# A decoder layer on one core: norms of tokens from a second load of x, squared and summed along rows by ScalarE

## The chip, the cores and the metric

One core of a Trainium2 chip runs the whole program. The metric is device time of one execution in microseconds (us), lower is better. The engines are TensorE (PE in the profile, with PEld for its weight loads), VectorE (DVE), ScalarE (ACT), GpSimd (POOL) and SyncE (SP, which here only issues DMAs and loads registers). Each engine works through its own list of instructions in order, and semaphores hold an instruction until what it reads is there and what it overwrites is free.

## The reference, cut to what matters

One decoder layer over a prompt of 1024 tokens and 8 single-token decode sequences, 1024 features. Its first step is an RMS norm of each token and one wide projection; keys, values, queries and gates come out of the projection.

```python
def rms_norm(x, g):
    xf = x.astype(jnp.float32)
    y = xf * lax.rsqrt(jnp.mean(xf * xf, axis=-1, keepdims=True) + EPS)
    return (y * g.astype(jnp.float32)).astype(x.dtype)
...
q, kc, ks, kw, gl, za, pin, zb, u, v, zc = project(rms_norm(xp, norm_pre[l]), w_in[l])
```

The change concerns only the number `mean(xf * xf)` of each token, for the prompt and for the 8 decode tokens.

## The kernel before

Features lie on partitions: `xT` is loaded as eight tiles of 128 features by 1032 tokens (1024 of the prompt and 8 to decode). The projection is made without the norm, and the norm is multiplied in afterwards, by a tile `R` that holds 1/sqrt of each token's mean square in all partitions.

For float32 precision each tile of x is split into two float16 parts, `xh` (ScalarE) and `xl` (VectorE, `split_x`, lines 277 and 278), each weight tile likewise (`split_k`, `split_w`), and three products are added in PSUM, in three chunks of 344 columns (`t_mms`). The program begins with two weight groups side by side, the keys `G_KSK` and `G_KWK`, in the order in which the eight tiles of x arrive (loop at line 412; `k_mms`). They fill `pa[0]`, `pa[1]`, `pf[0]` and `pf[1]`, whose results ScalarE copies to `tk` (line 457). Then come, group by group, the values `G_KSV` (first by name `t2` in the rows below, PSUM `ps2_0`, `ps2_1`, `ps2_2`), `G_KWV` (`ps3`), the queries and so on (`tgroup`). `ps2_0` and `ps2_1` use the PSUM banks of `pf[0]` and `pf[1]`, and split weights (`ws`) have two buffers, so that those of `G_KSV` take the place of those of `G_KSK`.

The sums of squares of before: `sq_x` squares the tiles of x in place, 0, 2, 4, 6 and 7 on ScalarE with the sum on VectorE (lines 287 and 289), and 1, 3, 5 on GpSimd (lines 283 and 285); line 439 adds the two sums. The 128 partitions are added by nine products with a column of ones (line 445, `pq`). From there: `ssq` (VectorE), `rst` by a power of -1/2 (GpSimd, line 450), a diagonal `dg` (VectorE, line 459), two products with ones that bring it to all partitions (`bcast`, `pr`), and ScalarE's copy to `R` (line 474). `R` then multiplies `tk` (line 484, VectorE); `post_k` makes float16 parts and issues DMAs from GpSimd, and `post_v` fills `vh`, clears its rest by a memset on GpSimd (line 508) and has SyncE transpose it by DMA (line 510).

SyncE and GpSimd keep the order in which the program is written (`manual_schedule`); TensorE, VectorE and ScalarE have an order that a scheduler worked out when the program was built. On SyncE, behind the loads of the start and the load of a weight group (line 243), stand 32 loads of page numbers into registers (line 296), then the next weights, the transposing DMA, and the loads of cache pages (`cr`, line 311), which GpSimd, ScalarE, TensorE and VectorE work on next (`dec_cmp`). Tiles named `t32` share five buffers.

Of the kernel before, what the change touches and what calls it, by code (L numbers as in the profile page):

```python
# [17 lines left out]
NT = 1032  # L18
# [32 lines left out]
def tile_hymba(ctx: ExitStack, tc: tile.TileContext, A: dict):  # L51
# [14 lines left out]
    def mm(out, l, r, st, en):  # L66
        nc.tensor.matmul(out, lhsT=l, rhs=r, start=st, stop=en)  # L67
# [148 lines left out]
    def t32(name, shape=None, dt=F32):  # L216
        return W.tile(shape or [128, NT], dt, tag="t32", name=name, bufs=5)
# [28 lines left out]
    def split_w(gi):  # L246
        raw = raws.pop(gi)
        if gi == "vg":
            ws = D.tile([128, 2, 8, 152], F16, tag="vs", name="wsvg", bufs=1)
            parts = ((raw[0], 0, 128), (raw[1], 128, 152))  # L250
        else:
            ws = X.tile([128, 2, 8, 128], F16, tag="ws", name=f"ws{gi}", bufs=2)
            parts = ((raw, 0, 128),)
        for r, a, b in parts:
            S.activation(ws[:, 0, :, a:b], r, AF.Copy, scale=64.0)  # L255
            if "attn" in hold:
                later(3.8)
                G.tensor_scalar(r, r, 64.0, None, ALU.mult)  # L258
                G.tensor_tensor(ws[:, 1, :, a:b], r, ws[:, 0, :, a:b], ALU.subtract)
            else:  # L260
                V.scalar_tensor_tensor(ws[:, 1, :, a:b], r, 64.0, ws[:, 0, :, a:b], ALU.mult, ALU.subtract)
        wsp[gi] = ws
# [14 lines left out]
        S.activation(xh[k], x, AF.Copy, scale=g)  # L277
        V.scalar_tensor_tensor(xl[k], x, g, xh[k], ALU.mult, ALU.subtract)

    def sq_x(k):  # L280
        x = xraw.pop(k)
        if k in (1, 3, 5):
            G.tensor_tensor(acc[1] if k == 1 else x, x, x, ALU.mult)
            if k > 1:
                G.tensor_tensor(acc[1], acc[1], x, ALU.add)
        else:
            S.activation(x if k else acc[0], x, AF.Square)
            if k:
                V.tensor_tensor(acc[0], acc[0], x, ALU.add)

    pgv = {}

# [61 lines left out]


    G.dma_start(cdt, A["cd"])
    acc = [t32("acc0"), t32("acc1")]
    wk = {}
    for gi, pl in ((G_KSK, RW), (G_KWK, D)):
        wk[gi] = (pl.tile([128, 8, 128], F32, tag="raw" if pl is RW else "rawd", name=f"raw{gi}", bufs=1),  # L360
# [40 lines left out]
    def k_mms(g, ws, k):  # L401
        for c in range(3):
            t_mms(g[c], ws, c, k, k == 0, k == 7)
# [8 lines left out]
    for k in range(8):  # L412
        if k == 0:
            split_k(G_KSK, 1, 4)
            split_k(G_KWK, 1, 4)
        if k == 2:
            split_k(G_KSK, 4, 8)
            split_k(G_KWK, 4, 8)
        if k < 7:
            split_x(k + 1)  # L420
        if k > 0:
            sq_x(k - 1)
        if k == 3:
            load_w(G_KSV)
            load_w(G_KWV)
            for q in range(3):
                load_sw(q)
            Y.dma_start(ptt, A["pt"])
        k_mms(g0, wk[G_KSK][1], k)
        if k < 6:  # L430
            k_mms(g1, wk[G_KWK][1], k)
    sq_x(7)
    for h, xx in ((0, xh), (1, xl)):
        for k in range(8):
            G.tensor_copy(xd[:, k, h], xx[k][:, 1024:NT])
    for h in range(2):
        G.tensor_copy(xdr[:, h].rearrange("p k (b h) -> p k b h", h=8),
                      xd[:, :, h].unsqueeze(3).to_broadcast([128, 8, 8, 8]))
    V.tensor_tensor(acc[0], acc[0], acc[1], ALU.add)
    split_w(G_KSV)  # L440
    k_mms(g1, wk[G_KWK][1], 6)
    k_mms(g1, wk[G_KWK][1], 7)
    pq = op.tile([128, 512], F32, tag="o", name="pq")
    for i in range(8):
        mm(pq[:, i:i + 1], acc[0][:, i * 128:i * 128 + 128], one1[:, 0:1], True, True)
    mm(pq[0:8, 8:9], acc[0][:, 1024:NT], one1[:, 0:1], True, True)
    ssd = D.tile([8, 1], F32, name="ssd")
    rsd = D.tile([8, 1], F32, name="rsd")
    V.tensor_scalar(ssq, pq[:, 0:8], 1.0 / 1024, EPS, ALU.mult, ALU.add)
    G.tensor_tensor(rst, ssq, nhalf[:, 0:8], ALU.pow)  # L450
    V.tensor_scalar(ssd, pq[0:8, 8:9], 1.0 / 1024, EPS, ALU.mult, ALU.add)
    G.tensor_tensor(rsd, ssd, nhalf[0:8, 0:1], ALU.pow)
    vnh = C.tile([128, 2, 8, 256], F16, tag="mxp", name="vnh")
    tk = [t32(f"tk{b}") for b in range(2)]
# [11 lines left out]
    Y.dma_start(bstt, A["cx"][:, 384:640])  # L466

    def bcast():
        for q in range(2):
            pr = op.tile([128, 512], F32, tag="o", name=f"pr{q}")  # L470
            mm(pr, one1, dg[:, q * 4:q * 4 + 4].rearrange("p a b -> p (a b)"), True, True)

            def done(q=q, pr=pr):
                S.activation(R[:, q * 512:q * 512 + 512], pr, AF.Copy)
                if q == 1:
                    V.tensor_copy(R[:, 1024:NT], pq[:, 16:24])
                    V.tensor_scalar(rsn, rst, -1.0 / 64, None, ALU.mult)
# [1345 lines left out]
```

## Time and profile before

| what | us |
|---|---|
| three timed runs | 608.07, 604.58, 608.36 (median 608.07) |
| the profiled execution, its own time | 602.71 |
| its span | 600.9 |
| busy: TensorE, VectorE, ScalarE, GpSimd | 537.8, 461.5, 323.9, 213.6 |

The profile is of one execution. Busy times are summed over stages with different limits, so a stage is read by its own rows: what an engine waited for, and which engine came last. Times in the rows count from the start of the span.

### The profile page before, as it was taken

The numbers are of one execution on the slowest core, as the hardware profiler recorded it, in microseconds if no ns is written. First come the engines' busy times: TensorE is split into PE (matmuls) and PEld (weight loads), VectorE is DVE, ScalarE is ACT, GpSimd is POOL, SyncE is SP. The second block draws the span as 40 slices with busy tenths as digits, with TensorE's granted clock in tenths as the row PEclk, the third lists the DMA queues.
The fourth block names the chain that finished last, engine by engine and source line by source line (L and its number), as shares of the span: only waits on it lengthen the run. The fifth ranks groups of instructions, "written<-read, shape, count | busy, mean of one in ns | idle before, by whom it ended". The sixth has DMA issues, their size and how long they took to land.

```text
span 600.9 us, 14161 instructions
## 1 busy us (share of the span) xinstructions
PE 537.8 (89%) x5716; PEld 348.4 (58%) x5716; DVE 461.5 (77%) x803; ACT 323.9 (54%) x576; POOL 213.6 (36%) x149
## 2 busy tenths in 40 slices
PE   5989989889999999989897987978657999999994
PEld 2656655579768998456565645645233644555551
DVE  5986489995785663578988999979978867877652
ACT  6444245464542443477666746657556747665510
POOL 1794288202446000363732566523943010000010
PEclk9999999998999999899998989989678799999998
DMA  8613884454634826289798878698996894996373
GB/s 299 245 35 121 237 223 129 117 158 126 211 131 131 286 73 170 63 137 189 126 192 165 153 145 124 117 143 193 189 237 122 129 218 104 179 212 155 80 158 122
DMA packets 196883, 95.29 MB, mean 159 GB/s; under 512 B 166866, under 2 KB 185714, under 8 KB 196754
## 3 DMA queue, kind: packets, MB, share of 16 engines
q1 hardware_dynamic: 194018, 81.37, 61.8%
q0 software_dynamic: 2656, 12.77, 6.3%
q8 instruction: 44, 0.72, 0.5%
q10 hardware_dynamic: 144, 0.26, 0.1%
q14 instruction: 21, 0.17, 0.1%
HBM read 45.43 MB, written 11.86 MB: 95 GB/s over the span
## 4 chain that ended last, share of the span: by engine, by line
PE 46%; DVE 21%; DMA 12%; issue 8%; SPq 8%; ACT 3%; POOL 1%; DVEq 0%; POOLq 0%; ACTq 0%
PE op L67 13%; PE ps L67 11%; PE s L67 7%; DMA T<-H 6%; PE zps L67 5%; PE O L67 4%; DVE H L1336 3%; DVE P L1326 3%; SPq L296 3%; PE v1ps L67 2%; DMA o_ps_dram<-dsh 1%; DMA xq<-in_xT_dram 1%; ACT H L1330 1%; SPq L318 1%; SPq L311 1%
## 5 line engine op out<-in xcount | busy, mean ns | idle before, releaser
L67 PE MATMUL ps<-xh,ws 128*128 128x344 f16 x768 | 178.4, 315 | 7.1 <-DVE t L492 4.8
L67 PEld LDWEIGHTS <-ws 128*128 128x128 f16 x1376 | 129.7, 100 | 89.8 <-issue 17.9
L1328 ACT ACTIVATE P<-P,sm 128x640 f32<-128x640 f32 (+7 forms) x128 | 92.9, 727 | 73.4 <-DVE sm L1326 73.1
L67 PE MATMUL ps<-xl,ws 128*128 128x344 f16 x384 | 120.9, 315 | 0.0
L1326 DVE CUSTOM_DVE_ANT_0 P<-s,ctt 128x640 f32<-128x640 f32 (+7 forms) x128 | 85.9, 701 | 12.2 <-PE s L67 11.2
L1336 DVE SCALAR_TENSOR_TENSOR H<-P,H 128x1024 f16<-128x1024 f32 (+4 forms) x50 | 83.5, 1670 | 14.5 <-ACT H L1330 14.5
L67 PEld LDWEIGHTS <-qa 128*128 128x128 f16 (+1 forms) x612 | 46.4, 98 | 80.3 <-issue 51.4
L1330 ACT ACTIVATE H<-P 128x1024 f16<-128x1024 f32 (+4 forms) x50 | 66.2, 1326 | 24.5 <-DMA T<-H 23.6
L67 PE MATMUL O<-vn,T 128*128 128x64 f16 x1584 | 61.7, 198 | 14.8 <-DMA T<-H 14.8
L67 PEld LDWEIGHTS <-T 128*128 128x128 f16 x1584 | 56.7, 101 | 24.8 <-DMA T<-H 16.3
L67 PE MATMUL s<-ka,qa 128*128 128x384 f16 (+4 forms) x192 | 54.4, 340 | 14.8 <-DVE sm L1326 14.5
L67 PEld LDWEIGHTS <-xh 128*128 128x128 f16 x768 | 61.3, 99 | 0.7
L67 PE MATMUL op<-wo,qa 128*128 128x512 f16 x192 | 46.1, 387 | 1.5 <-DMA qa<-yza 1.5
L67 PE MATMUL zps<-ws,xh 128*128 128x128 f16 x512 | 45.0, 219 | 0.0
L67 PE MATMUL zps<-ws,xl 128*128 128x128 f16 x256 | 43.6, 219 | 0.0
L1499 POOL TENSOR_SCALAR sq<-sq 128x1 f32<-128x1 f32 x8 | 2.6, 327 | 106.3 <-ACT o L1529 92.9
L67 PEld LDWEIGHTS <-xl 128*128 128x128 f16 x384 | 38.0, 99 | 2.7 <-issue 2.1
L258 POOL TENSOR_SCALAR raw<-raw 128x1024 f32<-128x1024 f32 x6 | 19.1, 3186 | 55.8 <-ACT ws L255 55.7
L67 PE MATMUL s<-kl,qa 64*128 64x384 f16 (+5 forms) x100 | 34.1, 348 | 0.0
L255 ACT ACTIVATE ws<-raw 128x1024 f16<-128x1024 f32 x21 | 22.2, 1056 | 16.4 <-PE ps L67 10.5
L67 PE MATMUL s<-klx,qx 64*128 64x384 f16 (+4 forms) x92 | 30.9, 335 | 0.0
L585 POOL TENSOR_TENSOR cr<-cr,pett 128x512 f32<-128x512 f32 x12 | 23.8, 2005 | 6.7 <-DMA cr<-in_ccmp_dram 6.1
(333 smaller groups left out, 946.3 us busy)
## 6 DMA issues: line engine op xcount, KB each, us to landing
raw<-in_wt_dram SPq DMA_DIRECT2D x21, 512.0 KB, 4.1
wor<-in_wo_dram POOLq DMA_DIRECT2D x8, 512.0 KB, 5.8
xr<-in_xn_dram SPq DMA_DIRECT2D x8, 512.0 KB, 4.4
o_kww_dram<-in_cwin_dram POOLq DMA_DIRECT2D x1, 4088.0 KB, 16.6
o_y_dram<-o SPq DMA_DIRECT2D x7, 512.0 KB, 3.7
cr<-in_ccmp_dram SPq DMA_DIRECT2D x24, 128.0 KB, 3.0
xq<-in_xT_dram SPq DMA_DIRECT2D x3, 516.0 KB, 8.4
kr<-in_cselk_dram SPq DMA_DIRECT2D x20, 64.0 KB, 2.0
```

Source lines behind the costliest of these rows:

```text
L67: nc.tensor.matmul(out, lhsT=l, rhs=r, start=st, stop=en)
L255: S.activation(ws[:, 0, :, a:b], r, AF.Copy, scale=64.0)
L258: G.tensor_scalar(r, r, 64.0, None, ALU.mult)
L296: pgv[n] = Y.value_load(ptt[0:1, n:n + 1], min_val=0, max_val=39)
L311: Y.dma_start(t[:, :, j * 128:(j + 1) * 128], A["ccmp"][page(b, j)].rearrange("o p (r c) -> (o p) r c", r=2))
L318: Y.dma_start(t[:, 0, j * 128:(j + 1) * 128], A["csel" + kv][page(b, j)].rearrange("o p c -> (o p) c"))
L585: G.tensor_tensor(xv, xv, pet[:, r].unsqueeze(1).to_broadcast([128, 8, 64]), ALU.add)
L1326: V.tensor_tensor_reduce(p, ps[:, z:z + T], ctt[:, end - T:end], -slope, 3e38, ALU.add, ALU.min, sm[:, s, br:br + 1])
L1328: S.activation(p, p, AF.Exp, bias=sm[:, s, br:br + 1], scale=-1.0, accum_out=sm[:, s, 2 + br:3 + br])
L1330: S.activation(H[:, 0], P, AF.Copy, scale=1024.0)
L1336: V.scalar_tensor_tensor(H[:, 1], P, 1024.0, H[:, 0], ALU.mult, ALU.subtract)
L1499: G.tensor_scalar(sq[:, 2:3], sq[:, 1:2], 1.0 / 1024, sq[:, 0:1], ALU.mult, ALU.add)
```

## The change

The nine sums of squares come from a second load of x, this time with tokens on partitions (`xn`, 1024 by 1024, and `xs`, 8 by 1024, both in memory already). Nine loads on SyncE fill tiles `xsq` of 128 tokens by 1024 features, taken from the five `t32` buffers, and one instruction of ScalarE per tile squares it and gives the sum of each row (`accum_out`) into a column of `ssn`. The squares of `sq_x`, the additions on VectorE and GpSimd and the nine products with ones are gone, and `ssq` reads `ssn`. The first product of `bcast` is asked for one step later (`yield 0.0`).

```diff
-    def sq_x(k):
-        x = xraw.pop(k)
-        if k in (1, 3, 5):
-            G.tensor_tensor(acc[1] if k == 1 else x, x, x, ALU.mult)
-            if k > 1:
-                G.tensor_tensor(acc[1], acc[1], x, ALU.add)
+    xsq = {}
+
+    def load_n(i):
+        xsq[i] = t32(f"xsq{i}", [128, 1024])
+        if i < 8:
+            Y.dma_start(xsq[i], A["xn"][i * 128:(i + 1) * 128])
         else:
-            S.activation(x if k else acc[0], x, AF.Square)
-            if k:
-                V.tensor_tensor(acc[0], acc[0], x, ALU.add)
+            Y.dma_start(xsq[i][0:8], A["xs"])
+
+    def sq_n(i):
+        t = xsq.pop(i)
+        if i < 8:
+            S.activation(t, t, AF.Square, accum_out=ssn[:, i:i + 1])
+        else:
+            S.activation(t[0:8], t[0:8], AF.Square, accum_out=ssn[0:8, 8:9])
...
-    acc = [t32("acc0"), t32("acc1")]
+    ssn = D.tile([128, 9], F32, name="ssn")
...
-        if k > 0:
-            sq_x(k - 1)
         if k == 3:
...
             Y.dma_start(ptt, A["pt"])
+            for i in range(3):
+                load_n(i)
+        if k > 4:
+            load_n(k - 2)
+            sq_n(k - 5)
...
-    sq_x(7)
...
-    V.tensor_tensor(acc[0], acc[0], acc[1], ALU.add)
     split_w(G_KSV)
+    for i in range(3, 9):
+        if i < 6:
+            load_n(i + 3)
+        sq_n(i)
     k_mms(g1, wk[G_KWK][1], 6)
     k_mms(g1, wk[G_KWK][1], 7)
     pq = op.tile([128, 512], F32, tag="o", name="pq")
-    for i in range(8):
-        mm(pq[:, i:i + 1], acc[0][:, i * 128:i * 128 + 128], one1[:, 0:1], True, True)
-    mm(pq[0:8, 8:9], acc[0][:, 1024:NT], one1[:, 0:1], True, True)
...
-    V.tensor_scalar(ssq, pq[:, 0:8], 1.0 / 1024, EPS, ALU.mult, ALU.add)
+    V.tensor_scalar(ssq, ssn[:, 0:8], 1.0 / 1024, EPS, ALU.mult, ALU.add)
...
     def bcast():
+        yield 0.0, None
         for q in range(2):
```

What the scheduler made of it on ScalarE, from the last split of x (`xh7`) to the first copies of `G_KSV`'s results; `ws2` and `ws3` are the split weights of `G_KSV` and `G_KWV`, and what an instruction waits for stands in brackets. Before:

```order
L277 ACTIVATE xh7_124<-xm_97,cdt_83 128x1032 [waits DMAHW6_49]
L287 ACTIVATE xm_97<-xm_97 128x1032 [waits DVE_49] x2
L346 ACTIVATE swl_137<-swr0_267 128x832 [waits DMAHW2_49]
L346 ACTIVATE wpl_111<-swr1_269 128x256 [waits DMAHW3_49]
L457 ACTIVATE tk0_419<-pa0_175 128x344 [waits PE_49]
L457 ACTIVATE tk0_419<-pa0_175 128x344
L255 ACTIVATE ws2_381<-raw2_263 128x1024 [waits DMAHW0_49,PE_49]
L457 ACTIVATE tk0_419<-pf0_177 128x344
L352 ACTIVATE wst_86<-swr2_271 128x512 [waits DMAHW4_49,DVE_49]
```

And now, from the split of the weights `ws2`:

```order
L255 ACTIVATE ws2_380<-raw2_258 128x1024 [waits DMAHW0_49,DVE_49,PE_49]
L292 ACTIVATE xsq0_269,ssn_147<-xsq0_269 128x1024 [waits DMAHW6_49]
L357 ACTIVATE wst_86<-swr2_266 128x512 [waits DMAHW4_49,DVE_49]
L292 ACTIVATE xsq1_271,ssn_147<-xsq1_271 128x1024 [waits DMAHW7_49]
L255 ACTIVATE ws3_437<-raw3_260 128x1024 [waits DMAHW1_49,PE_49,Activation_49]
L292 ACTIVATE xsq2_273,ssn_147<-xsq2_273 128x1024 [waits DMAHW0_49]
L292 ACTIVATE xsq3_315,ssn_147<-xsq3_315 128x1024 [waits DMAHW1_49]
L292 ACTIVATE xsq4_338,ssn_147<-xsq4_338 128x1024 [waits DMAHW2_49,Activation_49]
L464 ACTIVATE tk0_421<-pf0_176 128x344 [waits Activation_49]
L292 ACTIVATE xsq5_350,ssn_147<-xsq5_350 128x1024 [waits DMAHW3_49]
L464 ACTIVATE tk0_421<-pa0_174 128x344 x2
L464 ACTIVATE tk1_422<-pf1_177 128x344 [waits Activation_49]
```

Both splits of weights now stand ahead of the copies of `pf0`, and five squares as well; the remaining squares (`xsq6`, `xsq7`, `xsq8`) stand between these rows and the copy of `ps2_0`.

On SyncE, between the load of the page table and the load of the fifth weight group (`raw4`), before:

```order
L428 DMA ptt_142<-in_pt_dram 1x32 [waits DMAHW5_49]
L463 DMA cpt_81<-in_cp_dram 128x308 [waits DMAHW6_49]
L464 DMA pett_136<-in_cx_dram 128x128 [waits DMAHW7_49]
L465 DMA gnb_85<-in_cx_dram 128x256 [waits DMAHW0_49]
L466 DMA bstt_84<-in_cx_dram 128x256 [waits DMAHW1_49]
L243 DMA raw4_438<-in_wt_dram 128x1024 [waits DMAHW2_49,DVE_49]
```

And now, from the fourth of the new loads:

```order
L285 DMA xsq3_315<-in_xn_dram 128x1024 [waits DMAHW1_49]
L285 DMA xsq4_338<-in_xn_dram 128x1024 [waits DMAHW2_49,DVE_49]
L285 DMA xsq5_350<-in_xn_dram 128x1024 [waits DMAHW3_49,Activation_49]
L285 DMA xsq6_383<-in_xn_dram 128x1024 [waits DMAHW4_49,Activation_49]
L285 DMA xsq7_386<-in_xn_dram 128x1024 [waits DMAHW5_49,Activation_49]
L287 DMA xsq8_389<-in_xs_dram 8x1024 [waits DMAHW6_49,Activation_49]
L470 DMA cpt_81<-in_cp_dram 128x308 [waits DMAHW7_49]
L471 DMA pett_136<-in_cx_dram 128x128 [waits DMAHW0_49]
L472 DMA gnb_85<-in_cx_dram 128x256 [waits DMAHW1_49]
L473 DMA bstt_84<-in_cx_dram 128x256 [waits DMAHW2_49]
L243 DMA raw4_440<-in_wt_dram 128x1024 [waits DMAHW3_49,DVE_49]
```

Nine loads stand ahead of the others, and the last four of them wait for ScalarE's squares of `xsq0` to `xsq3`, whose buffers they take. The 32 loads of page numbers follow on `raw4` as before. On TensorE the first product of `bcast` (`pr0`) stood between the last products of `ps2_1` and now stands behind the fifth product of `ps2_2`; the second (`pr1`) stood within `ps2_2` and now stands behind its last.

## Rows read from the trace of the kernel before

**Rows 1.** Page, busy times, and busy time of each engine by stretch of the span (busy us and number of instructions per engine, then granted clock, DMA share, GB/s).
```profile
PE 537.8 (89%) x5716; PEld 348.4 (58%) x5716; DVE 461.5 (77%) x803; ACT 323.9 (54%) x576; POOL 213.6 (36%) x149
...
60.00:75.00 15.00, 14.97 (x104) 9.96 (x102) 5.92 (x8) 3.67 (x5) 3.33 (x4) 1.00 0.88 238
...
90.00:120.00 30.00, 27.44 (x186) 17.23 (x185) 29.81 (x32) 15.85 (x17) 16.43 (x9) 0.97 0.46 124
...
150.00:200.00 50.00, 50.00 (x572) 38.29 (x570) 34.94 (x54) 21.53 (x39) 21.89 (x9) 1.00 0.55 180
```
**Rows 2.** The chain of waits in order of time, from 31 to 77 us (start, length, what; the rows left out between 38.78 and 60.06 are the 32 loads of page numbers, L296).
```profile
31.47 1.23 DVE acc L289
...
37.29 1.15 DVE ws L261
38.45 0.33 SPq L243
...
38.84 0.47 SPq L296
...
60.06 0.34 SPq L243
60.51 6.25 SPq L510
...
72.73 2.55 DMA cr<-in_ccmp_dram
...
75.68 1.57 POOL cr L585
```
**Rows 3.** Timeline from 10 to 39 us (start, length, engine, line, operation, in brackets idle time before and its releaser): splits of x, GpSimd's squares, and TensorE at the end of the two key groups.
```profile
11.39 1.85 DVE L278 SCALAR_TENSOR_TENSOR xl<-xr,cdt,xh 128x1032 f16<-128x1032 f32 x1 [2.26 <-ACT xh L277]
13.16 1.28 DVE L278 SCALAR_TENSOR_TENSOR xl<-xq,cdt,xh 128x1032 f16<-128x1032 f32 x1
13.29 0.45 PE L67 MATMUL pa<-xl,ws 128*128 128x344 f16 x1 [1.14 <-DVE xl L278]
...
27.23 3.23 POOL L285 TENSOR_TENSOR acc<-acc,xr 128x1032 f32<-128x1032 f32 x1
28.16 3.39 DVE L278 SCALAR_TENSOR_TENSOR xl<-xm,cdt,xh 128x1032 f16<-128x1032 f32 x1
31.60 0.31 PE L67 MATMUL pa<-xl,ws 128*128 128x344 f16 x1 [2.50 <-DVE xl L278]
...
35.24 0.31 PE L67 MATMUL pf<-xh,ws 128*128 128x344 f16 x1
...
35.47 2.07 PE L67 MATMUL pq<-one,acc 128*128 128x1 f32 x18
...
38.48 0.47 PE L67 MATMUL ps<-xh,ws 128*128 128x344 f16 x2 [0.54 <-DVE ws L261]
```
**Rows 4.** Timeline of ScalarE: its copies at the end of the key groups, and, later in the program, instructions with and without a sum per row.
```profile
34.32 1.05 ACT L255 ACTIVATE ws<-raw 128x1024 f16<-128x1024 f32 x1
...
35.27 0.46 ACT L457 ACTIVATE tk<-pf 128x344 f32<-128x344 f32 x1
...
36.99 0.63 ACT L352 ACTIVATE wst<-swr 128x512 f16<-128x512 f32 x1 [1.27 <-DVE swr L351]
...
478.11 1.06 ACT L1330 ACTIVATE H<-P 128x1024 f16<-128x1024 f32 x1 [0.46 <-DMA T<-H]
479.07 0.71 ACT L1328 ACTIVATE P<-P,sm 128x512 f32<-128x512 f32 x1
479.69 0.19 ACT L1328 ACTIVATION_READ_ACCUMULATOR P<-P,sm 128x1 f32 x1
479.78 0.71 ACT L1328 ACTIVATE P<-P,sm 128x512 f32<-128x512 f32 x1
```
**Rows 5.** Timeline of SyncE around the four small loads, and its waits of the first 40 us (total, times, longest); then two DMA groups (KB each, median us from issue to landing), of the eight loads of x with tokens on partitions late in the program and of two loads of xT in the full queue of the start.
```profile
19.21 0.36 SPq L463 DMA_DIRECT2D cpt<-in_cp_dram  x1
...
23.06 0.33 SPq L466 DMA_DIRECT2D bstt<-in_cx_dram  x1
...
SPq L243 <- DVE ws L261: 14.3, 1, 14.3
...
xr<-in_xn_dram SPq DMA_DIRECT2D x8, 512.0 KB, 4.4
...
xm<-in_xT_dram SPq DMA_DIRECT2D x2, 516.0 KB, 9.0
```
**Rows 6.** TensorE's clock by stretch (columns as in rows 1; the clock is the third number from the end).
```profile
9.50:13.20 3.70, 1.41 (x7) 0.65 (x6) 1.81 (x2) 2.88 (x4) 1.90 (x1) 1.00 1.04 417
13.20:16.60 3.40, 3.31 (x12) 1.72 (x12) 3.40 (x5) 2.98 (x4) 0.00 (x0) 0.51 1.02 415
16.60:29.00 12.40, 12.40 (x86) 8.22 (x84) 12.40 (x7) 5.92 (x6) 10.74 (x4) 1.00 0.66 244
29.00:31.60 2.60, 0.11 (x1) 0.00 (x0) 2.60 (x2) 0.02 (x1) 2.60 (x3) 1.00 0.00 0
31.60:35.20 3.60, 3.60 (x25) 2.44 (x25) 3.39 (x3) 3.60 (x6) 3.60 (x7) 1.00 0.00 0
```
**Rows 7.** Timeline from the norms to the first transposing DMA.
```profile
41.63 1.68 POOL L450 TENSOR_TENSOR rst<-ssq,nhalf 128x8 f32<-128x8 f32 x1
...
43.34 1.23 DVE L459 TENSOR_TENSOR dg<-cet,rst 128x1024 f32<-128x1024 f32 x1 [2.15 <-POOL rst L450]
...
49.21 1.02 PE L67 MATMUL pr<-dg,one 128*128 128x512 f32 x2
...
50.27 0.60 ACT L474 ACTIVATE R<-pr 128x512 f32<-128x512 f32 x1 [3.15 <-PE pr L67]
...
50.90 2.38 DVE L484 TENSOR_TENSOR tk<-tk,R 128x1032 f32<-128x1032 f32 x2 [3.20 <-ACT R L474]
...
53.19 1.22 DVE L261 SCALAR_TENSOR_TENSOR ws<-raw,ws 128x1024 f16<-128x1024 f32 x1
...
59.35 0.34 POOL L508 MEMSET vh<- 128x240 f16 x1
```

More of the change, by code (lines that the diff above doesn't have):

```diff
@@ L443, in tile_hymba @@
     pq = op.tile([128, 512], F32, tag="o", name="pq")
-    for i in range(8):
-        mm(pq[:, i:i + 1], acc[0][:, i * 128:i * 128 + 128], one1[:, 0:1], True, True)
-    mm(pq[0:8, 8:9], acc[0][:, 1024:NT], one1[:, 0:1], True, True)
     ssd = D.tile([8, 1], F32, name="ssd")
     rsd = D.tile([8, 1], F32, name="rsd")
-    V.tensor_scalar(ssq, pq[:, 0:8], 1.0 / 1024, EPS, ALU.mult, ALU.add)
+    V.tensor_scalar(ssq, ssn[:, 0:8], 1.0 / 1024, EPS, ALU.mult, ALU.add)
     G.tensor_tensor(rst, ssq, nhalf[:, 0:8], ALU.pow)
-    V.tensor_scalar(ssd, pq[0:8, 8:9], 1.0 / 1024, EPS, ALU.mult, ALU.add)
+    V.tensor_scalar(ssd, ssn[0:8, 8:9], 1.0 / 1024, EPS, ALU.mult, ALU.add)
     G.tensor_tensor(rsd, ssd, nhalf[0:8, 0:1], ALU.pow)
```

## The prediction

> **What bounds the kernel now.** I read the busy times first, then the chain of waits, then the timeline of the first 75 us, since the change touches nothing later. TensorE is busy for 537.8 of 600.9 us [rows 1], which looks like its kernel; but the limits change by stage. From 150 to 200 us TensorE is never idle; from 90 to 120 VectorE is busy for 29.81 of 30 us; from 60 to 75 VectorE has 5.92 of 15 and TensorE is full [rows 1]. A delay ahead of a stage that is full to the brim is carried through it, and so is a gain.
>
> The chain of waits tells which engine hands the early delay on [rows 2]. It goes through VectorE's sums of squares, then VectorE's split of G_KSV's weights, which ends at 38.4, then SyncE: the load at 38.45, the 32 loads of page numbers up to 60, the transposing DMA at 60.51, the cache pages that land at 75.3, and GpSimd's work on them at 75.68. So what counts early on is when SyncE comes to line 243 (38.45 now; it had waited 14.3 us for VectorE there [rows 5]) and when `vh` is ready for the transposing DMA. The second is close behind: GpSimd's memset of `vh` ended at 59.69 [rows 7], 0.8 us before the DMA issued. TensorE's products alone aren't on this chain between 38 and 75 us.
>
> **What it removes.** GpSimd's squares slow VectorE down: a split of x takes 1.28 us alone and 1.85 or 3.39 us beside them [rows 3]. Without them and without the additions, `xl1` is ready 0.57 us earlier (1.85 less 1.28), and TensorE's wait of 2.50 us for `xl7` goes [rows 3]: x7 was in SBUF by 19.2 (SyncE's line 463 had waited for its load [rows 5]), so ScalarE's split ends at 20.3 and VectorE's by 21.7 if each follows at once, and TensorE gets there only near 28.5. The key products, which ended at 35.24 + 0.31 = 35.55, end 3.1 us earlier, at 32.4. The nine products with ones (2.07 us) and the wait for `ws` behind them go too. If G_KSV's products followed at once, at 32.4 in place of 38.48 [rows 3], TensorE would gain 6.1 us.
>
> **Where that gain goes.** They can't follow at once. `ps2_0` takes the PSUM bank of `pf0`, and on ScalarE the copy of `pf0` now stands behind both weight splits and five squares. The first split waits until TensorE is through with G_KSK, near 29.8 (nine products at 12.40/86 = 0.144 us behind the wait that ended at 31.60, plus the 0.31 us of the last, is 32.9; less 3.1) [rows 3, 6]. One square with a sum: an instruction of 1024 columns starts the next 0.96 us later (478.11 to 479.07), and one with a sum costs 0.09 more between its reading of the sum at 479.69 and the next start at 479.78 [rows 4]; I take 1.05 us. From below it is 0.96 (the reading free), from above 1.06 + 0.19 = 1.25 (nothing overlaps). Split 0.96, square 1.05, `wst` 0.54 (0.63 less the overlap of 0.09), square 1.05, split 0.96, three squares 3.15: 29.85 + 7.7 = 37.55, and the copy of `pf0` (0.46 [rows 4]) ends at 38.0. So TensorE begins G_KSV at 38.05, against 38.48 now: 0.4 us of the 6.1 is left, and the rest is a new wait of 5.65 us.
>
> That wait has a price of its own. Of 9.50 to 13.20 TensorE was busy for 1.41 us, and the clock granted afterwards was 0.51 for 3.40 us, 12 products where 0.144 us apiece is 24 [rows 6]; after the idle 2.50 us at 29 it stayed at 1.00 [rows 6]. The new gap is more than twice the latter, so I take the drop: 12 products at 0.283 (3.40/12) instead of 0.144, 1.7 us. From below it is nothing. The Trainium skill, "TensorE: Matmul & The Clock Gate", section "What's actually happening", states that the throttled clock is the default and that activity releases it; by that rule the drop is certain here, and by the row at 29 us alone it would not come. The sum by the one is +2.3 us and by the other +0.7, both worked out below from rows.
>
> **The norms.** After `pf0` ScalarE has square, two copies, copy, square, two copies, two squares (the last on 8 partitions but as long), which ends at 38.0 - 0.1 + 5.9 = 43.8; the eighth square ends near 42.85. Then `ssq` 0.15, `rst` 1.68, `dg` 1.23 [rows 7]: `dg` is ready at 45.95 (44.57 now). TensorE comes to `pr0` after two chunks of 24 products and five more: 38.05 + 53 x 0.144 = 45.7, or 47.4 with the drop. `pr0` takes 1.0, 19 products 2.75, `pr1` 1.0: 50.7, or 52.15. ScalarE copies `ps2_2` and splits `ws4` beside that, and `R` (0.60 [rows 7]) ends near 51.8, or 53.4, against 50.87 now. VectorE's split of `ws4` (1.22), which stood behind `tk` at 53.19, now stands ahead of it, so that `tk` times `R` starts at 52.4, or 54.0, not at 50.90: +1.5 or +3.1 us. From there to the end of the memset is 59.69 - 50.90 = 8.8 us of `kh`, GpSimd's ten DMA issues and the memset, unchanged: 61.2, or 62.8. The transposing DMA goes at 61.25 or 62.85, not 60.51: **+0.7 or +2.3 us**.
>
> **SyncE's own line.** Nine loads stand ahead. The first five wait only for earlier loads and are out by about 25 us, since SyncE issued its four small loads between 19.21 and 23.4 with the same waits [rows 5]. `xsq5` to `xsq8` wait for squares 0 to 3, the last of which ends near 36.6. Then `xsq8`, four small loads of 0.33 to 0.36 us and the gaps between them, and `raw4` goes at about 38.8, against 38.45: +0.35. The load itself is as cheap as a wait, because what VectorE is late with now has gone. Behind it the 21.6 us of page loads end at 60.4, so the transposing DMA still waits for `vh`. Do the late loads land in time? Such loads took 4.4 us [rows 5]; `xsq5`, issued at 31.9, lands at 36.3 and is wanted at 37.9; `xsq6` and `xsq7` (33.5 and 35.5) land at 37.9 and 39.9, wanted at 40.0 and 41.7. They cost nothing at 4.4 us and are 3 us late at 9.0, the time in the full queue of the start [rows 5]; that queue is empty by then except for these loads.
>
> **The sum.** +2.3 us, through the cache pages into VectorE's full stage and TensorE's full stage [rows 1], where I see nothing to swallow it, since their order hardly changed. On the profiled execution: 602.71 + 2.3 = 605.0. The four executions shown (602.71, 604.58, 608.07, 608.36) have a mean of 605.9, and I put the forecast on that: **608.2 us**.
>
> **The rivals.**
> First, the clock holds through the gap: +0.7, 606.6. For it speaks the 2.50 us gap at full clock, against it that the new one is twice as long.
> Second, faster: ScalarE squares the tiles as they land, while it waits for TensorE from 21.7 to 29.8, so that the squares don't block the copies. The fourth tile, issued by 23.1 as the last small load is now, lands by 32.1 even at 9.0 us [rows 5]; squared by 33.2, it would let SyncE come to line 243 near 35.4, about 3 us before 38.45, and with TensorE 6.1 us ahead `vh` would keep up: 602.9. It decides once three squares move ahead of the first split; the order has them behind, so only a much shorter square or an earlier G_KSK does any of it.
> Third, slower by more: the loads that wait for squares take 9 us, and each square behind `xsq4` is late by 3 us; `R` comes 3 us later, and with the drop of the clock the sum is +5.3, 611.2. The 4 MB of extra load in a stretch that had 0.00 of DMA share [rows 6] speaks against it. Were a square 1.25 us too, eight of them ahead of `dg` add 1.6: 612.8, which is just over 1%.
> Fourth, nothing: the delay is swallowed by slack in SyncE's and VectorE's waits between 60 and 90 us: 606.
>
> **How the numbers follow.** Chances: the forecast 0.5, the clock held or the delay swallowed 0.27, faster 0.08, slower by the late loads 0.15. About 1%, 6 us, is what a measurement of this kernel can tell from no change. The fastest case is 3 us below 605.9, so more than 1% faster gets 0.04, for what I don't see; more than 1% slower takes two thirds of the last rival, 0.10. Range: from 602 (the fast rival, less 1 for the fastest execution shown, at 602.71) to 613.5 (the slow one, on a median like 608.4).
>
> **What would show it.** In the profile after: key products that end near 32.4 with no wait for `xl7`; then TensorE idle for over 5 us with ScalarE (line 464) as releaser; half clock behind it; `R` done at 53.4; the transposing DMA at 62.9; line 243 at 38.8. If G_KSV starts well before 38, squares are shorter or placed otherwise than I read; if line 243 comes late, the loads were slow; if the DMA is at 62.9 and the total hasn't moved, the later stages have slack that I didn't find.

## The result, and the profile after

| | kernel before | changed kernel |
|---|---|---|
| median of 20 runs each, one chip (us) | 607.17 | 611.08 |
| median on a second chip (33 and 10 runs) | 606.45 | 610.23 |
| time against the kernel before, first chip | 1 | 1.0069, 95% interval 1.0043 to 1.0095 |
| the same on the second chip | 1 | 1.0056, 95% interval 1.0020 to 1.0092 |
| span of the profiled execution | 600.9 | 609.8 |

Ratios leave out runs over 1.5% above the fastest of their kernel, so they differ a little from those of the medians. The change costs 3.4 to 4.2 us (0.0056 and 0.0069 of 605; the intervals reach from 1.2 to 5.7 us): within 1%, on the slow side. The forecast of 2.3 us is less than both, just outside the first interval and inside the second.

The changed kernel's timeline from 28 to 78 us (columns as in [rows 3] and [rows 7]):

```profile
30.17 0.31 PE L67 MATMUL pf<-xh,ws 128*128 128x344 f16 x1
...
33.35 0.18 ACT L292 ACTIVATION_READ_ACCUMULATOR xsq<-xsq 128x1 f32 x1
33.44 1.04 ACT L292 ACTIVATE xsq<-xsq 128x1024 f32<-128x1024 f32 x1
...
34.48 1.04 ACT L292 ACTIVATE xsq<-xsq 128x1024 f32<-128x1024 f32 x1
...
35.64 0.46 ACT L464 ACTIVATE tk<-pf 128x344 f32<-128x344 f32 x1
...
36.15 0.45 PE L67 MATMUL ps<-xh,ws 128*128 128x344 f16 x1 [5.67 <-ACT tk L464]
...
36.80 19.63 SPq L243 DMA_DIRECT2D raw<-in_wt_dram  x2
...
42.94 1.23 DVE L466 TENSOR_TENSOR dg<-cet,rst 128x1024 f32<-128x1024 f32 x1 [0.84 <-POOL rst L457]
...
51.82 0.59 ACT L482 ACTIVATE R<-pr 128x512 f32<-128x512 f32 x1
...
53.84 2.36 DVE L492 TENSOR_TENSOR tk<-tk,R 128x1032 f32<-128x1032 f32 x2
...
61.56 0.52 POOL L509 DMA_DIRECT2D ka<-kh  x1 [0.92 <-DMA ka<-kh]
...
62.99 0.32 POOL L516 MEMSET vh<- 128x240 f16 x1
63.33 5.01 SPq L518 DMA_TRANSPOSE vn<-vh  x1
...
73.81 0.30 POOL L516 MEMSET vh<- 128x240 f16 x1 [7.92 <-DMA vn<-vh]
```

Key products end at 30.5, five us before [rows 3]; TensorE then idles 5.67 us until ScalarE copies `pf0`, which stands behind squares that follow each other every 1.04 us. `R` is done at 52.4, the transposing DMA goes at 63.33 (60.51 in [rows 2]). The second memset of `vh` waits for that DMA to land, so its start, 73.81, tells the landing. Two later milestones are used below: the first page product, GpSimd's first work on a cache page (`cr` from `cr` and `pett`, 75.49 here), and the first product of `zps`, a later group of products on TensorE.

TensorE's clock in the same execution (columns as in [rows 6]):

```profile
0.00:20.00 20.00, 13.69 (x74) 8.07 (x75) 12.72 (x23) 13.48 (x17) 2.27 (x12) 1.00 0.88 328
...
31.00:36.00 5.00, 0.00 (x0) 0.00 (x0) 1.46 (x2) 4.97 (x11) 0.00 (x0) 0.91 0.89 249
36.00:42.00 6.00, 5.85 (x21) 3.03 (x21) 0.21 (x2) 5.93 (x14) 0.77 (x1) 0.51 0.70 231
42.00:46.00 4.00, 4.00 (x30) 2.68 (x28) 1.83 (x8) 0.46 (x1) 1.43 (x2) 1.00 0.00 2
```

After the idle stretch the clock is at its lower level (1.2 of 2.4 GHz): 21 products in 5.85 us, 0.279 apiece, against 30 in 4.00 at the upper one.

From the chain of waits, in order of time: ScalarE's squares, TensorE behind them and GpSimd's loads of `ka` now lead to the transposing DMA, where VectorE and SyncE's page numbers did in [rows 2]; the last row is the first product of `zps`, in the stage that TensorE fills.

```profile
33.35 2.27 ACT xsq L292 x5
36.15 10.70 PE ps L67 x53
...
56.45 4.82 DMA ka<-kh
63.33 5.01 SPq L518
...
75.34 3.06 DMA draw<-in_ccmp_dram
...
190.52 2.68 PE zps L67 x48
```

### The profile page after: what moved, and what is told of

Same layout as the page of the kernel before. It is cut to its first block, busy times and chain, and to the rows that moved or that the text cites. A ratio compares the mean times of both kernels' runs of the same rounds, so it can differ in the third digit from the quotient of the medians.

```text
span 609.8 us, 14138 instructions
## 1 busy us (share of the span) xinstructions
PE 536.5 (88%) x5698; PEld 349.2 (57%) x5698; DVE 448.8 (74%) x798; ACT 328.5 (54%) x589; POOL 193.9 (32%) x144
## 4 chain that ended last, share of the span: by engine, by line
PE 52%; DVE 18%; DMA 15%; issue 5%; ACT 4%; SPq 4%; POOL 2%; DVEq 0%; POOLq 0%; ACTq 0%
PE ps L67 15%; PE op L67 12%; DMA T<-H 9%; PE s L67 7%; PE zps L67 5%; PE O L67 4%; DVE H L1344 3%; DVE P L1334 2%; PE v1ps L67 2%; PE pa L67 2%; ACT H L1338 1%; DMA qa<-yza 1%; DVE qa L528 1%; DMA xr<-in_xT_dram 1%; SPq L316 1%
## 5 line engine op out<-in xcount | busy, mean ns | idle before, releaser
L67 PE MATMUL ps<-xh,ws 128*128 128x344 f16 x768 | 181.7, 320 | 17.5 <-DVE t L500 8.2
L1336 ACT ACTIVATE P<-P,sm 128x640 f32<-128x640 f32 (+7 forms) x128 | 92.9, 727 | 73.0 <-DVE sm L1334 72.7
L67 PE MATMUL ps<-xl,ws 128*128 128x344 f16 x384 | 122.9, 320 | 0.0
L67 PE MATMUL s<-ka,qa 128*128 128x384 f16 (+4 forms) x192 | 52.5, 329 | 10.0 <-DVE sm L1334 9.9
L67 PE MATMUL s<-kl,qa 64*128 64x384 f16 (+5 forms) x100 | 32.9, 336 | 0.0
L593 POOL TENSOR_TENSOR cr<-cr,pett 128x512 f32<-128x512 f32 x12 | 21.7, 1829 | 10.8 <-DMA cr<-in_ccmp_dram 10.5
```

The source lines that it names most:

```text
L593: G.tensor_tensor(xv, xv, pet[:, r].unsqueeze(1).to_broadcast([128, 8, 64]), ALU.add)
L1336: S.activation(p, p, AF.Exp, bias=sm[:, s, br:br + 1], scale=-1.0, accum_out=sm[:, s, 2 + br:3 + br])
```

## The experiments

Theory A is the prediction's: copies stand behind squares, TensorE idles, its clock falls, `R` and the first transposing DMA come late, and that is passed on. B: the second loads of x cost, by SyncE's waits or by traffic. C: the scheduler's moved rows (instructions that now stand elsewhere in an engine's order) cost something later. One table of all milestones stands at the end of the section.

**Without the empty step.**
```diff
     def bcast():
-        yield 0.0, None
```


> The changed kernel without the one empty step ahead of the broadcast (line 476); the loads and the squares stay. Order now: both products with dg stand back to back behind the fifth group of ps2_2, both copies into R stand ahead of ScalarE's split of ws4, and tk times R ahead of VectorE's split of ws4. Theory A (copies of the key sums stand behind squares, TensorE idles, the clock falls, R comes late) expects: gap of about 5.7 us and the half clock stay; R done near 49 in place of 52.4, transposing DMA near 61 in place of 63.3, so 1.5 to 2.5 us off the changed kernel, about 609 (ratio to before 1.003 to 1.005). Theory C (the extra step reorders VectorE's full stage at 75 to 120 us, which costs the other 2 us) expects that the first value product's milestones lose more than the transposing DMA gains, 4 us in all, ratio near 1.000. Theory B (SyncE's loads come late) expects no change, ratio 1.007.


Measured: transposing DMA at 60.31, as A had it, but 1.0101 (1.0046 to 1.0157). A fails at its end: the DMA is on time and the kernel no faster. Nor did it go as C had it. The kernel isn't clean, though: without the step the scheduler moves rows all through attention (VectorE's order differs from before's in 43 places in the last 60% of its instructions; the changed kernel's in 17).

**Copies first.**
```diff
                 load_n(i)
+            tk = [t32(f"tk{b}") for b in range(2)]
...
     split_w(G_KSV)
+    k_mms(g1, wk[G_KWK][1], 6)
+    k_mms(g1, wk[G_KWK][1], 7)
+    for gg, t in ((g0, tk[0]), (g1, tk[1])):
+        for c in (2, 0, 1):
+            S.activation(t[:, c * CH:c * CH + CH], gg[c], AF.Copy, scale=1.0 / 64)
     for i in range(3, 9):
...
-    k_mms(g1, wk[G_KWK][1], 6)
-    k_mms(g1, wk[G_KWK][1], 7)
...
-    tk = [t32(f"tk{b}") for b in range(2)]
-    for gg, t in ((g0, tk[0]), (g1, tk[1])):
-        for c in (2, 0, 1):
-            S.activation(t[:, c * CH:c * CH + CH], gg[c], AF.Copy, scale=1.0 / 64)
```


> The changed kernel with the six copies of the key sums ahead of squares four to nine in the program, and the two tk tiles taken from their pool before the later tiles of x. SyncE's order of loads and the empty step stay. Theory A expects: no gap over 2 us in TensorE at 30 to 37 us, the granted clock at 1.00 up to 46, ps2 done near 42, R set by the last square and dg and done near 46 to 48, the transposing DMA near 58 to 59: 4 us off the changed kernel, about 607 (ratio to before near 1.000). Theory B (late loads on SyncE) expects no gain, ratio 1.007. Theory C expects the transposing DMA earlier, but the time in VectorE's stage at 75 to 120 us to be lost again, ratio 1.003 to 1.005.


Measured: 1.0198 (1.0138 to 1.0258), the slowest of all; every theory missed. TensorE's idle time fell to 3.44 us, no further. What took its place, in SyncE's timeline, and then in the chain of waits:

```profile
38.74 0.30 SPq L287 DMA_DIRECT2D xsq<-in_xs_dram  x1
...
40.94 21.77 SPq L243 DMA_DIRECT2D raw<-in_wt_dram  x2
```

```profile
60.29 0.80 SPq L301
62.81 13.75 DMA vn<-vh
76.66 1.07 ACT vh L265
```

The late loads wait for squares that now stand behind the copies, so SyncE issues `raw4` at 40.94; its 32 page numbers end near 62.2, and the DMA goes at 62.81 though `vh` was ready at 61.94. Once issued it takes 13.75 us. SyncE's own lateness makes 0.9 us (62.81 for 61.94), and most of the 12 us that this kernel loses isn't in these rows: the DMA goes between the two times of the changed kernel (63.33 and 60.67), and `zps`, at 191.65, is 1.1 to 3.2 us later than there.

**No second load, no squares; and the loads alone.**
```diff
+    V.memset(ssn, 1024.0)
...
-            for i in range(3):
-                load_n(i)
-        if k > 4:
-            load_n(k - 2)
-            sq_n(k - 5)
...
-    for i in range(3, 9):
-        if i < 6:
-            load_n(i + 3)
-        sq_n(i)
```


> Leaves out part of the computation: the second loads of x and the squares are gone, and a constant stands for the sums of squares; everything behind them stays. It is the ceiling of what the norm costs. Theory A and B both expect dg done by 30, no gap in TensorE, R near 45, the transposing DMA near 55 to 57, 6 to 8 us off the changed kernel if an earlier start passes through (about 603 to 605, ratio to before 0.993 to 0.996). If the late start is not what costs the time (theory C), ratio 1.002 or above.


```diff
-            S.activation(t, t, AF.Square, accum_out=ssn[:, i:i + 1])
+            S.activation(tch[:, i:i + 1], t[:, 0:1], AF.Square)
...
+    V.memset(ssn, 1024.0)
```


> Leaves out part of the computation: the nine loads of x stay, but of each tile only one column is squared (to release it), and a constant stands for the sums of squares. Theory A (ScalarE's time is what costs) expects this near the run without loads and squares, at most 1.5 us above it. Theory B (the loads: traffic beside the weights, SyncE's waits, raw4 issued late) expects it near the changed kernel, 4 us or more above the run without loads and squares.


Measured: 0.9988 (0.9952 to 1.0025) without both, 1.0063 (1.0025 to 1.0101) with the loads. So even with no norm at all and a transposing DMA 8.15 us early (52.36) no gain is clear of noise. That doesn't show that an early start is worth nothing: the interval reaches down to 0.9952, which is 2.9 us, and the medians of all runs, 602.89 against 605.63, are 2.7 us apart. The loads seem to cost 4.5 us (0.0075 of 605), as B had it; whether by SyncE or by traffic, a later pair asks.

**Late loads from ScalarE's queue.**
```diff
-            Y.dma_start(xsq[i], A["xn"][i * 128:(i + 1) * 128])
+            (Y if i < 5 else S).dma_start(xsq[i], A["xn"][i * 128:(i + 1) * 128])
...
-            Y.dma_start(xsq[i][0:8], A["xs"])
+            S.dma_start(xsq[i][0:8], A["xs"])
```


> The changed kernel with the last four loads of x issued from ScalarE's queue, so that SyncE waits for no square and comes to raw4 and to its 32 page numbers some 6 us earlier (raw4 at 30 to 32 in place of 36.8). In the changed kernel the transposing DMA waited 4.6 us for VectorE's vh, not for SyncE's own work; so if SyncE's lateness is not the cause (theory A), the transposing DMA stays at 62 to 64 and the ratio to before at 1.005 to 1.010. Theory B (SyncE's waits on squares are what costs): transposing DMA near 60.5 and ratio 1.000 to 1.003.


Measured: `raw4` at 30.46, transposing DMA at 62.42, ratio 1.0042 (1.0008 to 1.0077). SyncE wasn't the cause in the changed kernel: its DMA waited 11.4 us for VectorE's `vh`. The ratio is not told apart from the changed kernel's. This kernel also bears on theory C: by its trace, no instruction of VectorE, ScalarE or TensorE behind 186 us stands in another place than in the kernel before, and its interval lies above 1 all the same.

**All three together.** Copies first as above, and:
```diff
-            Y.dma_start(xsq[i], A["xn"][i * 128:(i + 1) * 128])
+            (Y if i < 3 else S).dma_start(xsq[i], A["xn"][i * 128:(i + 1) * 128])
...
-            Y.dma_start(xsq[i][0:8], A["xs"])
+            S.dma_start(xsq[i][0:8], A["xs"])
...
-        yield 0.0, None
```


> Copies of the key sums ahead of the late squares, late loads of x from ScalarE's queue, no empty step ahead of the broadcast. The copies-first run came out slower, and its trace shows SyncE at raw4 only at 40.9, its page numbers done at 62.2 and the transposing DMA at 62.8 behind them, not behind vh. If SyncE's chain of squares, raw4 and page numbers took the place of the late R there, this kernel has raw4 near 30 to 33, R near 46 to 48, vh near 56 to 58 and the transposing DMA within 1 us of vh: first page product of GpSimd at 71 to 73, ratio to before 0.997 to 1.003. If the traffic of the second loads of x is what costs (the run with loads and without squares was 5 us above the one without either), ratio 1.005 to 1.010 although the transposing DMA is earlier than before's 60.5.


Measured: `raw4` at 31.40, but `R` at 50.87: the last squares waited 0.64 and 1.22 us for their loads, and the DMA went at 61.68. First page product 73.79, `zps` at 186.75, as early as the kernel before, and yet 1.0105 (1.0067 to 1.0142). By this one execution, what it loses lies behind 186 us, where the diff touches nothing (the scheduler's order differs from before's in 7 places there on VectorE).

**TensorE kept busy in the gap.**
```diff
     k_mms(g1, wk[G_KWK][1], 7)
+    wm = op.tile([128, 512], F32, tag="o", name="wm")
+    for i in range(32):
+        mm(wm[:, :CH], wk[G_KWK][1][:, 0, i % 8], xh[7][:, 0:CH], True, True)
```


> The changed kernel with 32 more products of 344 columns on TensorE behind the last key product, into a spare bank that nothing reads, so that TensorE is busy while ScalarE's copies stand behind squares. It also moves ScalarE's split of ws3 behind two squares. If the idle stretch is what took the clock down, the granted clock stays at 1.00 from 32 to 46, ps2 is done some 1.5 us earlier than in the changed kernel, R near 51 and the transposing DMA near 61.8. End to end that is 0 to 1.5 us off the changed kernel: ratio to before 1.004 to 1.008. If the clock falls all the same, nothing moves.


TensorE in the gap (timeline), and the clock (windows):

```profile
30.10 4.83 PE L67 MATMUL wm<-xh,ws 128*128 128x344 f16 x32
36.42 0.31 PE L67 MATMUL ps<-xh,ws 128*128 128x344 f16 x1 [1.49 <-ACT tk L467]
```

```profile
31.00:36.00 5.00, 3.93 (x27) 2.52 (x26) 0.01 (x1) 4.48 (x10) 0.00 (x0) 1.00 0.85 289
36.00:42.00 6.00, 5.58 (x39) 3.76 (x39) 1.40 (x2) 6.00 (x14) 0.51 (x1) 1.00 0.61 192
```

The clock held, so the idle stretch is what took it down (A's link stands): ScalarE's copies of `R` ended at 49.5, 2.9 us before the changed kernel's (1.6 before those of its second profile, below). The DMA still went at 62.85: `tk` waited until 52.48 for the last 8 columns of `R`, then GpSimd's `ka` for an earlier DMA. Ratio 1.0063 (1.0027 to 1.0098).

**The kernel before, profiled again, and the changed kernel again.**


> The kernel before, profiled once more, to see how far one execution's milestones carry: first page product of GpSimd (72.5 in the first profile), first product of zps (186.2), span 600.9. If the stretches up to 190 are the same in each execution and what scatters lies behind them (attention, with its clock), the two milestones repeat within 1 us and the span moves by up to 6 us.

> The changed kernel once more. If one execution's milestones carry up to 75: transposing DMA within 0.7 of 63.3, first page product of GpSimd within 0.5 of 75.5. If what was added between 75 and 190 in the first profile (zps at 190.5 in place of 186.2) is scatter between executions, as the second profile of the kernel before had it (188.3), zps comes at 188 to 190.5. Ratio 1.004 to 1.009.


The kernel before, second profile (GpSimd's timeline, then the chain of waits):

```profile
71.23 0.30 POOL L508 MEMSET vh<- 128x240 f16 x1 [6.66 <-DMA vn<-vh]
72.78 5.35 POOL L585 TENSOR_TENSOR cr<-cr,pett 128x512 f32<-128x512 f32 x3 [1.25 <-DMA cr<-in_ccmp_dram]
```

```profile
188.33 2.68 PE zps L67 x48
```

TensorE's idle time at 31 us in the same execution (timeline), and the clock in two stretches of [rows 6] (windows):

```profile
31.30 0.31 PE L67 MATMUL pa<-xl,ws 128*128 128x344 f16 x1 [3.27 <-DVE xl L278]
```

```profile
13.20:16.60 3.40, 3.40 (x25) 2.28 (x24) 3.40 (x5) 2.99 (x4) 0.00 (x0) 1.00 1.03 421
...
31.60:35.20 3.60, 3.60 (x16) 1.97 (x14) 3.39 (x4) 3.60 (x7) 3.60 (x7) 0.53 0.00 0
```

The changed kernel, second profile (timelines, then TensorE's clock, then the chain of waits):

```profile
50.45 0.59 ACT L482 ACTIVATE R<-pr 128x512 f32<-128x512 f32 x1
60.67 6.77 SPq L518 DMA_TRANSPOSE vn<-vh  x1
73.64 2.70 POOL L593 TENSOR_TENSOR cr<-cr,pett 128x512 f32<-128x512 f32 x2 [1.68 <-DMA cr<-in_ccmp_dram]
```

```profile
31.00:36.00 5.00, 0.19 (x1) 0.11 (x1) 1.22 (x1) 4.97 (x11) 0.00 (x0) 0.66 0.81 267
36.00:42.00 6.00, 6.00 (x31) 3.46 (x30) 0.31 (x2) 5.92 (x14) 1.11 (x1) 0.71 0.63 204
```

```profile
188.43 2.68 PE zps L67 x48
```

One execution's milestones carry less far than thought. The kernel before repeats within 0.7 us at the DMA's issue and 0.3 at its landing and the first page product; then `zps` scatters by 2.1 us and the span by 7.2 (600.9 and 608.1). The clock doesn't repeat either: in [rows 6] it fell at 13 us and not behind the idle 2.50 us at 29, and in the second profile of the same kernel it stayed at 1.00 at 13 us and fell to 0.53 behind an idle 3.27 us. In the changed kernel the lower clock fell half into the idle time the second time (31 products in 36 to 42, not 21), so `R` came 1.4 us earlier. The transposing DMA came 2.7 us earlier; the other 1.3 us are GpSimd's, whose last issue of `ka` waited for an earlier DMA in the first profile and not in the second. The expectation of 63.3 missed. Mean of two: `zps` at 189.5, against 187.3 before.

**The kernel before with a late transposing DMA.**
```diff
+    dly = D.tile([128, 1024], F32, name="dly")
...
+        if b == 0:
+            for _ in range(6):
+                G.memset(dly, 0.0)
         G.memset(vh[:, :, NT:1152], 0.0)
```


> The kernel before with six fills of a spare 128x1024 tile on GpSimd right ahead of the first fill of vh, so that the first transposing DMA is issued late and nothing else of the norms changes. From fills in the first profile (0.10 us for one column, 0.20 for 128) one is an estimated 0.9 us, six 5.6: transposing DMA near 65.5 in place of 60.5. If a late transposing DMA is passed on one to one, as the prediction had it: first page product of GpSimd near 77.5 in place of 72.5, zps 5 later, ratio to the kernel before 1.008. If the stage behind takes it in: first page product later by under 2 us, ratio under 1.003. Above 1.012: it grows on the way.


GpSimd's and SyncE's timeline:

```profile
59.11 6.04 POOL L511 MEMSET dly<- 128x1024 f32 x6
65.09 0.30 POOL L512 MEMSET vh<- 128x240 f16 x1
65.41 4.40 SPq L514 DMA_TRANSPOSE vn<-vh  x1
71.59 0.30 POOL L512 MEMSET vh<- 128x240 f16 x1 [5.71 <-DMA vn<-vh]
75.18 4.53 POOL L589 TENSOR_TENSOR cr<-cr,pett 128x512 f32<-128x512 f32 x2 [3.29 <-DMA cr<-in_ccmp_dram]
```

Issued 4.9 us late by the first profile of the kernel before, the DMA landed 0.55 us late, by 71.6, not 71.04: it took 6.2 us instead of 10.5. The first page product is 2.7 us late. It doesn't wait for this DMA to land but for the page loads, which SyncE issues behind the DMA's own issue, 3.1 us late (SyncE's timeline, the kernel before and then this one):

```profile
66.98 6.29 SPq L311 DMA_DIRECT2D cr<-in_ccmp_dram  x8
```

```profile
70.04 5.82 SPq L311 DMA_DIRECT2D cr<-in_ccmp_dram  x8
```

`zps` at 188.5 is 0.2 us behind the later profile of the kernel before and 2.3 behind the earlier, the ratio 0.9986 (0.9955 to 1.0017). So part of the 4.9 us reaches the first page product, more than the 2 us of the second expectation, and none is seen in the time.

**The loads alone, late ones from ScalarE's queue.** The two edits above together.


> Leaves out part of the computation, as the run with loads and without squares: of each second tile of x only one column is squared, a constant stands for the sums. Now the last four tiles are loaded from ScalarE's queue. In the run with all loads on SyncE raw4 came at 34.1 and the transposing DMA at 57.1, straight behind SyncE's last page number, while vh was ready at 54.7. If SyncE's wait was what the loads cost there, raw4 comes near 30, the transposing DMA at 53 to 55 right behind vh, and the first page product of GpSimd near 70; ratio 0.998 to 1.001 as without loads. If it was their traffic, the transposing DMA stays at 56 or later, or takes its 3 us longer to land, and the ratio stays at 1.005 to 1.007.


Measured: 0.9983 (0.9953 to 1.0012), not told apart from the 0.9988 of the run without loads. So the 4 MB of traffic isn't seen to cost anything, though the DMA went late, at 59.35, as expected for traffic. It waited 6.8 us for VectorE's `vh` and landed in 7.2 us; `zps` at 182.78. SyncE's order would then be what the loads cost before, but that kernel, unlike this one, also had rows moved in attention (31 places on VectorE against 3), and the two aren't told apart.

**The empty step alone, in the kernel before.**
```diff
     def bcast():
+        yield 0.0, None
```


> The kernel before with nothing but the empty step ahead of the broadcast: some rows of VectorE and ScalarE change places, most of them ahead of 100 us, two behind 250. It shows what moved rows alone do. If the step matters in itself, R and the first page product move by 1 us or more against 72.5 and the ratio leaves 0.998 to 1.002; if what the run without the step lost was the many rows that it moved in attention, this one stays at 1.000.


Measured: 1.0065 (1.0019 to 1.0110), as much as the whole change. The DMA's issue and landing (timelines), and the DMA engines beside it (windows):

```profile
60.28 8.00 SPq L511 DMA_TRANSPOSE vn<-vh  x1
74.68 0.30 POOL L509 MEMSET vh<- 128x240 f16 x1 [11.13 <-DMA vn<-vh]
```

```profile
66.00:68.00 2.00, 1.94 (x14) 1.17 (x12) 0.91 (x1) 1.06 (x1) 0.00 (x0) 1.00 1.21 219
68.00:70.00 2.00, 1.14 (x8) 0.77 (x8) 1.29 (x3) 0.00 (x0) 0.00 (x0) 1.00 1.77 110
```

Issued between the two times of the kernel before (60.51 and 59.80), it took 14.4 us, not 10.5 or 11.4. `R` is done at 51.08, 0.2 us later than before. The rows that the step moves there are ScalarE's, VectorE's and TensorE's around `R`; GpSimd's first store now goes at 53.57, not 52.44.

All milestones in us. Landing is the start of the second memset of `vh`; the clock is the mean granted clock of the runs in the ratio, for the kernel before that of its last series (0.946 and 0.943 in two earlier ones). Each ratio is to the kernel before in the same series, and series differ: "loads only" and "late loads from ScalarE" have the same median, 608.01.

| kernel | DMA issued | landed | first page product | first `zps` | ratio | clock |
|---|---|---|---|---|---|---|
| before, two profiles | 60.51, 59.80 | 71.04, 71.23 | 72.51, 72.78 | 186.21, 188.33 | 1 | 0.944 |
| changed, two profiles | 63.33, 60.67 | 73.81, 71.66 | 75.49, 73.64 | 190.52, 188.43 | 1.0069, 1.0056 | 0.940 |
| without the step | 60.31 | 70.44 | 73.69 | 187.83 | 1.0101 | 0.935 |
| copies first | 62.81 | 76.67 | 79.63 | 191.65 | 1.0198 | 0.933 |
| no loads, no squares | 52.36 | 67.26 | 69.36 | 181.84 | 0.9988 | 0.943 |
| loads only | 57.10 | 68.81 | 72.06 | 184.53 | 1.0063 | 0.938 |
| late loads from ScalarE | 62.42 | 71.12 | 74.68 | 187.66 | 1.0042 | 0.938 |
| all three | 61.68 | 71.10 | 73.79 | 186.75 | 1.0105 | 0.934 |
| clock held | 62.85 | 74.92 | 76.51 | 190.14 | 1.0063 | 0.941 |
| before, DMA late | 65.41 | 71.59 | 75.18 | 188.50 | 0.9986 | 0.944 |
| loads only, from ScalarE | 59.35 | 66.50 | 70.72 | 182.78 | 0.9983 | 0.935 |
| before, empty step | 60.28 | 74.68 | 76.18 | 189.26 | 1.0065 | 0.942 |

By these ratios no version is measurably faster than the kernel before; the three lowest all have 1 in their interval.

## Why the prediction was right, and the step that the runs don't bear out

*What it removes.* Right in kind, too small: the key products end at 30.5, not 32.4. There is no wait for `xl7`, and the half-clock stretch of [rows 6] at 13 us didn't come either (granted clock 1.00 from 0 to 20). That can't be put down to the change: it didn't come in the second profile of the kernel before either.

*Where the gain goes.* Right: G_KSV's products begin at 36.15 behind an idle 5.67 us (forecast 5.65), with the named releaser. (The working has two slips: 31.60 + 9 x 0.144 + 0.31 is 33.2, not 32.9, and 52.15 + 0.60 makes `R` 52.75, not 53.4; neither decides anything.) Squares follow at 1.04 us (1.05). The two rows that the prediction weighed for the clock, a drop at 13 us and none at 29, gave no rule, since the second profile has them the other way round. The clock fell both times, at a cost of 21 x (0.279 - 0.144) = 2.8 us in the first profile and 6.00 - 31 x 0.144 = 1.5 in the second; 1.7 was forecast. The Trainium skill, "TensorE: Matmul & The Clock Gate", section "What's actually happening", has the throttled clock as the default that activity releases; the traces agree, 0.51 behind an idle gap and 1.00 where 32 products filled it.

*The norms.* Chain right, term about right: `R` done at 52.4 and 51.0 (forecast 53.4), the transposing DMA at 63.33 and 60.67 (62.85). Against the two profiles of before, 60.16 on average, that is +1.8 us, for +2.3. That the terms fit so closely is partly luck: G_KSV's products began 1.9 us earlier than forecast (36.15 for 38.05), and in the first profile the drop of the clock cost 1.1 us more than forecast and GpSimd's wait for a DMA of `ka` another 1.3.

*SyncE's own line.* Right: line 243 at 36.80 (38.8), the late loads landed in a median of 4.1 us (4.4 priced) and delayed no square; loads in ScalarE's queue changed nothing that can be told.

*The sum.* This step isn't borne out: "+2.3 us, through the cache pages into VectorE's full stage and TensorE's full stage [rows 1], where I see nothing to swallow it, since their order hardly changed". With the late DMA in the kernel before, 4.9 us at the issue are 0.55 at the landing, 2.7 at the first page product, 1.2 at `zps` against the mean of the two profiles, and none in the time. The run without norms has it the other way: 8.15 us earlier at the issue, 3.2 to 3.4 at the first page product, 4.4 to 6.5 at `zps`, and no gain clear of noise at the end (2.7 us by the medians of all runs). So a shift of the transposing DMA is passed on in part, not one to one. And the order did matter: the empty step, whose moved rows I costed at nothing, by itself makes the kernel before as slow as the changed one (1.0065), with `R` only 0.2 us later.

So the +2.3 us came out near the truth without the path that was given for it being shown. `zps` is indeed 2.2 us later in the changed kernel, by the mean of two profiles each, but one unchanged kernel scatters by 2.1 there. What the twelve kernels have in common is told by two numbers: how late `zps` begins, and how long TensorE runs at the lower clock, which is (1 - clock) x 2 x time, since that level is half. A least-squares fit over the table's twelve kernels (mean of two profiles where there are two) gives 0.70 us per us of `zps` and 0.48 us per us at the lower clock, and is off by 1.4 us (root mean square), at most by 3, in times that spread over 13. For the changed kernel: `zps` 2.2 us later, 1.5 us; 72.7 us at the lower clock against 67.5, 2.5 us; together 4.0, measured 3.4 and 4.2. By it the forecast counted the first term and missed the second. This is an association of few points, not a cause that was switched on and off, and two things on record weaken it. Within the kernel before alone, three series of 23, 26 and 33 runs give only 0.24 to 0.33 us per us at the lower clock. And the four profiles don't show the second term: the granted clock of the whole span is 0.948 and 0.930 before, 0.943 and 0.945 in the changed kernel. Most of the time at the lower clock lies far behind the change: from 300 to 600 us the granted clock is 0.90 to 0.92 in these four, in the stretches ahead of it 0.95 to 0.98.

*Rivals.* "The clock holds" fell; "faster" fell (the squares stand where the order had them); "slower by late loads" fell in the changed kernel, where no square waited for its load; in the copies-first kernel two squares did, 1.7 us at most, and the late loads held up SyncE; "swallowed" was right in part for a late transposing DMA and missed that something else costs.

What stays open: why the same DMA takes 6 to 15 us, why kernels with the same `zps` differ by 13 us at the lower clock ("all three" against before), and what costs the rest of the time. The number of moved rows doesn't tell it: behind 186 us VectorE's order differs from before's in 43 places without the step (1.0101), in 17 in the changed kernel (1.0069), in 7 in "all three" (1.0105), in 2 with the empty step alone (1.0065) and in none with late loads from ScalarE (1.0042). The effects don't add either: the step costs 0.65% in the kernel before, and taking it out of the changed kernel gains nothing.

## What to carry to other kernels

A late transfer isn't priced at its issue: follow it to the first instruction that waits for its data, and to what stands behind it in the same queue. Here 4.9 us of lateness at the issue were 0.55 at the landing, 2.7 at the page product that stood behind it, and nothing in the time. Before a milestone of one execution is blamed, profile the unchanged kernel twice: here `zps` moved by 2.1 us and the span by 7.2, and the clock fell in another stretch, with no edit at all. And when a scheduler orders the engines, run the order-only part of a change alone: here an edit that computes nothing cost as much as the whole change.

## What the runs showed of the hardware

The first transposing DMA, 128 x 2304 float16 each time, landed 6.2 to 14.9 us after its issue. In the run without norms the first took 14.8 and the second of the same size 4.7 (DMA from issue to landing, minimum, median, maximum):

```profile
DMA to landing us min/median/max: 4.7/9.8/14.8
```

In the run that issued it late the DMA engines had just drained (windows). The three that took longest, 13.9 to 14.9 us, have stretches of 2 us with a DMA share above 1.2 in which the bytes moved fall to 110 to 152 GB/s, as from 68 to 70 us with the empty step above. That a full queue is what makes the DMA slow wasn't tested by itself.

```profile
60.00:64.00 4.00, 4.00 (x30) 2.66 (x28) 1.24 (x1) 0.46 (x1) 3.77 (x5) 1.00 0.96 313
64.00:66.00 2.00, 2.00 (x15) 1.35 (x14) 0.00 (x0) 1.02 (x1) 1.82 (x4) 1.00 0.11 39
```

The Trainium skill, "DMA: Bandwidth & Descriptors", section "Latency and other measured facts", gives 261 GB/s for a DMA transpose whose middle dimension isn't contiguous; 590 KB would be an estimated 2.3 us by it. No run shows whether this DMA is of that kind. No run here came near: 4.7 us at best, 14.9 at worst, beside stores and page loads.

ScalarE's sum costs nearly nothing: the reading of the accumulator shows 0.18 us, but squares follow each other every 1.04 us, 0.08 more than the 0.96 of a plain instruction of 1024 columns [rows 4].
